# A two-layer encoder trunk: input, result and modulation weight with channels on partitions

## The chip, the cores and the metric

The kernel runs on one core of a Trainium2 chip, as one launch. The metric is the device time of that launch in microseconds (us). Six engine names occur: PE is TensorE's matrix multiply and PEld its loading of stationary operands, DVE is VectorE, ACT is ScalarE, POOL is GpSimd, SP is SyncE, which here only issues transfers (DMAs). A trailing q (SPq, ACTq) means the engine's instruction queue. On-chip memory has 128 partitions; a tile written 128x512 has 512 elements on each of them. PSUM is the memory that PE writes.

## The reference

```
c_act = silu(c)                                             # (1, 1024)
for l in range(2):
    mod = c_act @ w_ada[l] + b_ada[l]                       # (1, 6144)
    sh1, sc1, g1, sh2, sc2, g2 = split(mod, 6)
    h  = rms_norm(x, norm1_g[l]) * (1 + sc1) + sh1          # x: (1, 512, 1024)
    x  = x + g1 * mixer_sublayer(h, ...)                    # three token mixers, merged by gates
    h2 = rms_norm(x, norm2_g[l]) * (1 + sc2) + sh2
    gate, up = split(h2 @ w_ffn_in[l], 2)
    x  = x + g2 * ((silu(gate) * up) @ w_ffn_out[l])
return rms_norm(x, norm_f_g)
```

512 tokens, 1024 channels, everything in float32. `w_ada` is (2, 1024, 6144): 50 MB that are read once and used for a product with one vector, "the modulation". Its result is needed per channel. Most of the work is in the products with `w_in`, the three projections, `w_out` and the two FFN weights.

## The kernel before

**Layout of the body.** Inside the body the activations stand with channels on partitions: `k.xd` holds x as eight tiles of 128 channels by 512 tokens (`xt(kk)`). Every weight tile is split by `parts` into a high part (ACT, a cast) and a low part (DVE, a difference), and `three` multiplies with three matmuls, so one 128x128 block of a weight against 512 tokens is three matmuls of 512 columns. The matmuls of the whole kernel stand in PE's queue one behind the other; the body is a long stream of them, with the other engines preparing operands.

**The opening** (`first_products`, instructions of each engine in the order in which they are written, by `in_order`). The input arrives with tokens on partitions, as four tiles `xin` of 128x1024. ACT squares and sums each row (`sums`), DVE and POOL make the reciprocal root (`rstd`), DVE or ACT scale the rows (`scaled`), PE transposes them in 128x128 blocks (`turned`, L616) and they are copied to the channel layout `xr`. The modulation's first two groups (shift and scale of the first norm) are needed at once: for each channel tile kk a block of 1024x128 of `w_ada` is loaded twice (`fw`, once for each group, in pieces of 512 bytes); `columns` multiplies the one by `cact` on POOL and folds it to two 128x128 blocks (three POOL instructions, L624 and L626), and does the other with eight DVE instructions (L631, L633); `folded` adds over partitions with matmuls against a column of ones (L640). `tile` then makes shift and scale, applies them (L646, L648, L651), `split` makes the high and low part of h (L338, L339), and `products` runs the 18 matmuls of tile kk against the first three column blocks of `w_in` (banks `L0A0b`). From kk = 4 on `raw_x` puts transposes of the unscaled input between the matmuls (L656), so that `k.xd` has x in channel layout for the residual. The loads are issued by SP three tiles ahead; the buffer of a `w_in` block (`raw`, three of them) is reissued once the block has been split.

**The other ten groups of the modulation** (`mod_steps`) run in the background of the body, as 160 steps in the list `bg`. `weight`, which issues every weight load, also pops one or two steps (`k.rate`) while `k.ahead` allows it: two behind each weight load in the merge part of a layer, one in the FFN. A step loads 128 rows by 512 columns of `w_ada` (`wr`, 256 KB, two buffers, SP) and adds them, times `cact` for that partition, to `acc` on DVE (L208, L210). After eight steps, `fin` transposes `acc` with four PE transposes into PSUM (`mt`, L216), and DVE sums along rows (L218) and adds the bias (L220).

**Small vectors** (`arow`, `crow`, `prow`: biases, gains, bounds) are loaded as rows and turned by PE transposes.

**The seams.** Between sub-layers `boundary` runs the last two column blocks by halves of the tokens and the norm beside them: `squares` and `half_norm` (squares on ACT, sums over channels by matmuls with a column of ones, L423, the root on POOL, L352, then a diagonal matrix `dg`, L428, whose product with ones, L433, has 1/rms of each token on all partitions: `bc`). At the end, `last_norm` stops `half_norm` at the fifth of its seven steps, transposes x back to tokens on partitions (L1165), scales by 1/rms and by the gain `gf` (DVE, L1166, four 128x512 for each half) and writes 128 rows of the result with each of four DMAs (L1169).

**Buffers.** `duo` tiles (8 KB on each partition) come from a pool of 16; in the second part of each layer a further pool, `late`, has `LATE_DUOS` of the same size.

Outside `first_products` and the seam, the order of each engine is chosen when the program is built, by a scheduler that goes by program order as priority.

Of the kernel before, what the change touches and what calls it, by code (L numbers as in the profile page):

```python
# [11 lines left out]
F32 = mybir.dt.float32  # L12
# [3 lines left out]
ALU = mybir.AluOpType  # L16
# [22 lines left out]
R_N2, R_LB, R_NA, R_NB, R_NC, R_BA = 0, 16, 24, 32, 40, 48  # L39
R_END = 56  # L40

R_N1 = 96
R_EARLY = 112

# [5 lines left out]
LATE_DUOS = 4  # L50
# [66 lines left out]
def trunk_kernel(ctx: ExitStack, tc: tile.TileContext, a, out):  # L117
# [80 lines left out]
    def mod_steps(l, g):  # L198

        st = {}  # L200

        def row(hlf, kk):
            t = wp.tile([P, 512], F32, tag="ada", name=f"wr{l}_{g}_{hlf}_{kk}", bufs=2)
            c0 = g * DM + hlf * 512
            tc.keep_in_program_order(nc.sync.dma_start(t, a["w_ada"][l, kk * P:(kk + 1) * P, c0:c0 + 512]))
            if kk == 0:
                st["acc"] = wk.tile([P, 512], F32, tag="acc", name=f"acc{l}_{g}_{hlf}", bufs=1)
                nc.vector.tensor_scalar_mul(st["acc"], t, cact[:, 0:1])  # L208
            else:
                nc.vector.scalar_tensor_tensor(st["acc"], t, cact[:, kk:kk + 1], st["acc"],  # L210
                                               op0=ALU.mult, op1=ALU.add)

        def fin(hlf):
            ps = obank(f"mt{l}_{g}_{hlf}")
            for j in range(4):
                nc.tensor.transpose(ps[:, j], st["acc"][:, j * P:(j + 1) * P], ident)  # L216
            m = mod[l][:, g, hlf * 4:hlf * 4 + 4]
            nc.vector.tensor_reduce(m, ps, op=ALU.add, axis=AX.X)  # L218
            c0 = l * 48 + g * 8 + hlf * 4
            nc.vector.tensor_add(m, m, acol[:, c0:c0 + 4])  # L220
            if hlf:
                mod_finish(l, g)

        def step(hlf, kk):
            row(hlf, kk)
            if kk == KD - 1:
                fin(hlf)

        return [lambda hlf=hlf, kk=kk: step(hlf, kk) for hlf in range(2) for kk in range(KD)]
# [307 lines left out]
    def first_products():  # L537


        crow, arow = tmp("crow", (P, P)), tmp("arow", (P, P))  # L540
# [118 lines left out]
        for c in range(NCH):  # L659
            sums(c)  # L660
# [698 lines left out]
```

## Time and profile before

| | |
|---|---|
| median of three runs | 2006.54 us (2003.65 to 2008.01) |
| the profiled execution | 2004.59 us, its span 2002.8 us |
| PE busy | 1939.2 us, 97% |
| DVE / ACT / POOL busy | 1105.5 / 779.2 / 208.4 us |
| DMA | 231.95 MB, mean 116 GB/s |

"Busy" is the time in which an engine has an instruction in flight, "idle before" the time for which it stood still ahead of an instruction, with the event that ended it. The page cuts the span into 40 slices of 50 us. The opening is the first two of them, the merge parts of the layers lie at about 440 to 640 us and 1420 to 1610 us, the end is the last slice. A chain of waits, followed back from the last instruction, tells which work set the end.

### The profile page before, as it was taken

The page shows a single profiled execution, that of the slowest core. Times are in us where ns is not written, and L with a number is a line of the kernel's source. Part 1 is how long each engine was busy: PE and PEld are TensorE (multiplying, and loading weights), DVE is VectorE, ACT ScalarE, POOL GpSimd, SP SyncE. Part 2 cuts the span into 40 slices and gives each one's busy share as a digit, 9 for nine tenths or more (in the row PEclk, how much of TensorE's full clock was granted, in tenths as well). Part 3 has the DMA queues.
Part 4 walks back from the last instruction along what each step waited for, and adds up shares of the span by engine and source line. Part 5 has one row for each costly group of instructions (what it writes and reads, how often), then busy time and mean ns, then how long its engine had stood idle before and what let it go on. Part 6 is the DMA issues. An engine that isn't in the chain of part 4 may idle for free.

```text
span 2002.8 us, 32664 instructions
## 1 busy us (share of the span) xinstructions
PE 1939.2 (97%) x13507; PEld 1626.2 (81%) x13507; DVE 1105.5 (55%) x1797; ACT 779.2 (39%) x1298; POOL 208.4 (10%) x202
## 2 busy tenths in 40 slices
PE   5999999999999999999999999989999999999998
PEld 4898887777888888888889888777878888888887
DVE  7566576756635544453354756775764464434324
ACT  3543455633233433332244443654423353333222
POOL 6121011011110100000011201110111110000000
PEclk7999999999999999999999999999999999999999
DMA  8433212326633344443343322222564333333332
GB/s 248 144 100 92 77 57 85 107 97 190 187 95 118 103 129 155 139 145 116 116 125 89 105 76 67 75 93 78 178 195 122 95 122 126 111 99 101 101 95 79
DMA packets 208997, 231.95 MB, mean 116 GB/s; under 512 B 10720, under 2 KB 185104, under 8 KB 207824
## 3 DMA queue, kind: packets, MB, share of 16 engines
q1 hardware_dynamic: 207056, 224.80, 36.5%
q0 software_dynamic: 1504, 4.47, 0.8%
q8 instruction: 106, 1.74, 0.4%
q10 hardware_dynamic: 288, 0.58, 0.1%
q14 instruction: 43, 0.35, 0.1%
HBM read 221.43 MB, written 6.29 MB: 114 GB/s over the span
## 4 chain that ended last, share of the span: by engine, by line
PE 59%; issue 23%; DVE 7%; DMA 7%; ACT 1%; POOL 1%; SPq 0%; DVEq 0%; POOLq 0%; ACTq 0%
DMA wr<-w_ada 6%; DVE acc L210 1%; PE L0A0b L283 1%; PE L0A0b L284 1%; PE L0A0b L285 1%; DVE fw L633 1%; DMA fw<-w_ada 1%; PE L1fo2b L284 1%; PE L1fo1b L284 1%; PE L1fo0b L284 1%; PE L1fo1b L285 1%; PE L1fo0b L285 1%; PE L1fo2b L285 1%; PE L1fo2b L283 1%; PE L1fo1b L283 1%
## 5 line engine op out<-in xcount | busy, mean ns | idle before, releaser
L210 DVE SCALAR_TENSOR_TENSOR acc<-wr,cact,acc 128x512 f32<-128x512 f32 x140 | 106.1, 758 | 172.8 <-DMA wr<-w_ada 172.4
L352 POOL TENSOR_TENSOR L1h0r<-L1h0r,mhalf 128x2 f32<-128x2 f32 x1 | 1.1, 1079 | 348.4 <-DVE L1h0r L351 348.4
L352 POOL TENSOR_TENSOR fin0r<-fin0r,mhalf 128x2 f32<-128x2 f32 x1 | 0.7, 695 | 347.8 <-DVE fin0r L351 347.8
L338 ACT CAST L0hid<-L0fs 128x512 fp32r<-128x512 f32 x22 | 13.7, 622 | 31.9 <-DVE L0fs L1288 31.4
L633 DVE SCALAR_TENSOR_TENSOR fw<-fw,cact 128x128 f32<-128x128 f32 x48 | 23.2, 550 | 0.0
L218 DVE TENSOR_REDUCE mod<-mt 128x4 f32<-128x512 f32 x20 | 13.7, 686 | 15.0 <-PE mt L216 15.0
L640 PE MATMUL fm<-ones,fw 128*128 128x1 f32 x64 | 10.1, 278 | 11.9 <-DVE fw L633 9.1
L640 PEld LDWEIGHTS fm<-ones,fw 128*128 128x128 f32 x64 | 10.2, 237 | 13.9 <-DVE fw L633 10.1
L216 PE MATMUL mt<-ident,acc 128*128 128x128 f32 x80 | 13.3, 290 | 7.0 <-DVE acc L210 6.9
L1264 POOL TENSOR_TENSOR L1ma<-L1ma,L1sgb 128x512 f32<-128x512 f32 x6 | 10.1, 1704 | 92.9 <-DVE L1sgb L1263 92.9
L216 PEld LDWEIGHTS mt<-ident,acc 128*128 128x128 f32 x80 | 10.0, 148 | 11.4 <-issue 8.2
L651 ACT ACTIVATE xr<-xr,mod,gmul 128x512 f32<-128x512 f32 x8 | 6.5, 815 | 32.1 <-DVE gmul L648 32.1
L1264 POOL TENSOR_TENSOR L0ma<-L0ma,L0sgb 128x512 f32<-128x512 f32 x6 | 9.6, 1605 | 88.8 <-DVE L0sgb L1263 61.3
L624 POOL TENSOR_TENSOR fw<-fw,cact 128x1024 f32<-128x1024 f32 x8 | 17.0, 2120 | 11.9 <-DMA fw<-w_ada 11.9
L338 ACT CAST L1hid<-L1fs 128x512 fp32r<-128x512 f32 x22 | 13.7, 622 | 11.1 <-DVE L1fs L1288 10.0
L1264 POOL TENSOR_TENSOR L0ma<-L0ma,L0sgc 128x512 f32<-128x512 f32 x8 | 12.8, 1602 | 48.9 <-DVE L0sgc L1263 48.9
L1264 POOL TENSOR_TENSOR L1ma<-L1ma,L1sgc 128x512 f32<-128x512 f32 x8 | 12.4, 1559 | 47.1 <-DVE L1sgc L1263 47.1
L626 POOL TENSOR_TENSOR fw<-fw 128x512 f32<-128x512 f32 (+1 forms) x16 | 17.0, 1064 | 1.3
L339 DVE TENSOR_TENSOR L0hid<-L0fs,L0hid 128x512 fp32r<-128x512 f32 x22 | 15.1, 688 | 0.9
L339 DVE TENSOR_TENSOR L1hid<-L1fs,L1hid 128x512 fp32r<-128x512 f32 x22 | 15.2, 691 | 0.6
L767 DVE TENSOR_TENSOR L1AK<-L1AK,L1AG 128x1024 f32<-128x1024 f32 x12 | 14.6, 1216 | 0.7 <-POOL L1AG L759 0.7
L767 DVE TENSOR_TENSOR L0AK<-L0AK,L0AG 128x1024 f32<-128x1024 f32 x12 | 14.6, 1216 | 0.7 <-POOL L0AG L759 0.7
(5616 smaller groups left out, 6916.9 us busy)
## 6 DMA issues: line engine op xcount, KB each, us to landing
wr<-w_ada SPq DMA_DIRECT2D x160, 256.0 KB, 3.6
fw<-w_ada SPq DMA_DIRECT2D x16, 512.0 KB, 6.4
L0A0w<-w_in SPq DMA_DIRECT2D x8, 384.0 KB, 3.6
L0fo0w<-w_ffn_out SPq DMA_DIRECT2D x5, 512.0 KB, 4.0
L0fo1w<-w_ffn_out SPq DMA_DIRECT2D x5, 512.0 KB, 3.6
L0fo2w<-w_ffn_out SPq DMA_DIRECT2D x5, 512.0 KB, 3.5
L1hzw<-w_ffn_out SPq DMA_DIRECT2D x5, 512.0 KB, 3.5
L1fo0w<-w_ffn_out SPq DMA_DIRECT2D x5, 512.0 KB, 3.4
```

What stands on the lines that cost most here:

```text
L210: nc.vector.scalar_tensor_tensor(st["acc"], t, cact[:, kk:kk + 1], st["acc"], op0=ALU.mult, op1=ALU.add)
L216: nc.tensor.transpose(ps[:, j], st["acc"][:, j * P:(j + 1) * P], ident)
L283: nc.tensor.matmul(ps, ah, bh, start=first, stop=False, **kw)
L284: nc.tensor.matmul(ps, al, bh, start=False, stop=False, **kw)
L285: nc.tensor.matmul(ps, ah, bl, start=False, stop=last, **kw)
L338: nc.scalar.copy(h, src)
L339: return nc.vector.tensor_sub(dst[1][i // 2][:, i % 2], src, h.bitcast(F32))
L624: nc.gpsimd.tensor_mul(t, t, cact[:, :, None].to_broadcast([P, KD, P]))
L633: nc.vector.scalar_tensor_tensor(acc, t[:, j], cact[:, j:j + 1], acc, op0=ALU.mult, op1=ALU.add)
L640: nc.tensor.matmul(ps[:, g:g + 1], loads[kk][1 - g][:, j], ones[:, :1], start=j == 0, stop=j == 1)
L767: nc.vector.tensor_mul(kk, kk, crossed(t, s, d + 1, -d - 1, True))
L1264: nc.gpsimd.tensor_add(acc[i], acc[i], sg[i])
```

## The change

On the host, `x` and `w_ada` are transposed before the launch and the result behind it, and all small vectors are put side by side in one array `cols` of 128 x 176 in column form. In the kernel:

- x is loaded straight into `k.xd` (four DMAs of 512 KB). The transposes of `turned` and `raw_x`, and those of the small vectors, go.
- `cact` becomes 128x1024: c on all partitions. A piece of the modulation is then a dot product along rows: one DVE instruction over 128 channels by 512 inputs that also writes its row sum (`accum_out`). In `mod_steps` the steps stay 160, of the same 256 KB; `acc`, the transposes `mt` and the row reduction go. In the opening, each group's 128x1024 tile takes one DVE instruction with a sum (scale), or one POOL product and one ACT copy with a sum (shift).
- The first norm is done in channel layout: ACT squares, sums by matmuls with ones, POOL's root, the diagonal, `bc`; then for each tile one DVE instruction, one ACT instruction for the high part, one on DVE for the low part.
- The last norm runs `half_norm` to its end and multiplies in channel layout: eight DVE instructions of 128x256 for each half, and two DMAs of 512 KB.
- `LATE_DUOS` goes from 4 to 3; the pairs of `mg` and `hid` take one duo more each from the pool of 16, as does one tile of the seam between the layers.

```diff
-LATE_DUOS = 4
+LATE_DUOS = 3
...
+    cols = cst.tile([P, R_EARLY + R_END], F32, name="cols")
+    acol, pcol = cols[:, :R_EARLY], cols[:, R_EARLY:]
+    cact = cst.tile([P, DM], F32, name="cact")
...
     def mod_steps(l, g):
...
-        def fin(hlf):
-            ps = obank(f"mt{l}_{g}_{hlf}")
-            for j in range(4):
-                nc.tensor.transpose(ps[:, j], st["acc"][:, j * P:(j + 1) * P], ident)
...
+        def step(j, hlf):
...
+            t = wp.tile([P, 512], F32, tag="ada", name=f"wr{l}_{g}_{j}_{hlf}", bufs=2)
+            n0 = g * DM + j * P
+            tc.keep_in_program_order(nc.sync.dma_start(t, a["w_ada"][l, n0:n0 + P, hlf * 512:hlf * 512 + 512]))
+            nc.vector.scalar_tensor_tensor(t, t, 1.0, cact[:, hlf * 512:hlf * 512 + 512], op0=ALU.mult, op1=ALU.mult,
+                                           accum_out=st["sum"][:, hlf, j:j + 1])
...
     def first_products():
...
+        nc.scalar.dma_start(cact, a["c"].rearrange("o n -> (o n)").rearrange("(o n) -> o n", o=1).to_broadcast([P, DM]))
+        nc.scalar.dma_start(cols, a["cols"])
+        fresh_x("x")
+        for i in range(4):
+            nc.sync.dma_start(k.xd[i // 2][:, 2 * (i % 2):2 * (i % 2) + 2],
+                              a["x"][i * 2 * P:(i + 1) * 2 * P].rearrange("(j p) t -> p j t", p=P))
...
+            fd = duo(f"fw{kk}", shape=(P, 2, DM))
             for g in (1, 0):
...
+                nc.sync.dma_start(fd[:, g], a["w_ada"][0, g * DM + kk * P:g * DM + kk * P + P])
...
+        for i in range(2):
+            c, t = cact[:, i * 512:i * 512 + 512], tmp(f"cs{i}")
+            nc.scalar.activation(t, c, AF.Sigmoid)
+            nc.vector.tensor_mul(c, c, t)
+        def dots(kk):
+            fd = loads[kk][0]
+            nc.vector.scalar_tensor_tensor(fd[:, 1], fd[:, 1], 1.0, cact, op0=ALU.mult, op1=ALU.mult,
+                                           accum_out=mod[0][:, 1, kk:kk + 1])
+            nc.gpsimd.tensor_mul(fd[:, 0], fd[:, 0], cact)
+            nc.scalar.activation(fd[:, 0], fd[:, 0], AF.Copy, accum_out=mod[0][:, 0, kk:kk + 1])
+        def sums():
+            ps = obank("ssp", (P, 4))
+            for kk in range(KD):
+                sq = tmp(f"x0sq{kk}")
+                nc.scalar.activation(sq, xt(kk), AF.Square)
+                for c in range(NCH):
+                    nc.tensor.matmul(ps[:, c:c + 1], sq[:, c * P:(c + 1) * P], ones[:, :1], start=kk == 0 and c == 0,
+                                     stop=kk == KD - 1, skip_group_check=True)
+            r = rstd_of(ps, DM, "r0")
+            dg = tmp("x0dg", (P, 4, P))
+            nc.vector.tensor_tensor(dg, ident[:, None, :].to_broadcast([P, 4, P]),
+                                    r[:, :, None].to_broadcast([P, 4, P]), op=ALU.mult)
+            bc = obank("x0bc", (P, 4, P))
+            for c in range(NCH):
+                nc.tensor.matmul(bc[:, c], ones, dg[:, c], start=True, stop=True)
+            return bc.rearrange("p c t -> p (c t)")
+        bc = sums()
+        dots(0)
...
         def before(kk):
+            hl = [parts(loads[kk][1][:, :3, i * P:(i + 1) * P], f"L0A0w{kk}{i}") for i in range(2)]
             m = mod[0][:, 0:2, kk]
+            nc.vector.tensor_add(m, m, acol[:, 0:16].rearrange("p (g k) -> p g k", g=2)[:, :, kk])
             gm = gmul[0][:, 0, kk:kk + 1]
...
+            t, sh = tmp(f"x0t{kk}"), mod[0][:, 0, kk:kk + 1]
+            nc.vector.scalar_tensor_tensor(t, xt(kk), gm, bc, op0=ALU.mult, op1=ALU.mult)
+            hi, lo = h[0][kk // 2][:, kk % 2], h[1][kk // 2][:, kk % 2]
+            nc.scalar.activation(hi, t, AF.Identity, bias=sh)
+            nc.vector.scalar_tensor_tensor(lo, t, sh, hi.bitcast(F32), op0=ALU.add, op1=ALU.subtract)
+            if kk + 1 < KD:
+                dots(kk + 1)
             return hl
         def products(kk, i, hi, lo):
...
-            if kk >= NCH:
-                raw_x(kk - NCH, i)
...
     def last_norm(block, add):
...
+            for i in range(7):
+                bc = next(norm)
+            od = duo(f"out{hv}", shape=(P, KD, T // 2))
+            for kk in range(KD):
+                gf = pcol[:, R_NF + kk:R_NF + kk + 1]
+                nc.vector.scalar_tensor_tensor(od[:, kk], xt(kk)[:, half(hv)], gf, bc, op0=ALU.mult, op1=ALU.mult)
+                if kk % 4 == 3:
+                    dst = out[(kk - 3) * P:(kk + 1) * P, half(hv)].rearrange("(j p) t -> p j t", p=P)
+                    nc.sync.dma_start(dst, od[:, kk - 3:kk + 1])
```

More of the change, by code (lines that the diff above doesn't have):

```diff
@@ L200, in mod_steps @@
         st = {}
[L202 to L211, printed above, removed]
-        def fin(hlf):
-            ps = obank(f"mt{l}_{g}_{hlf}")
-            for j in range(4):
[L216 to L221, printed above, removed]
-                mod_finish(l, g)
[L224 to L229, printed above, removed]
+        def step(j, hlf):
+            if not st:
+                st["sum"] = sm.tile([P, 2, KD], F32, tag="msum", name=f"ms{l}_{g}")
+            t = wp.tile([P, 512], F32, tag="ada", name=f"wr{l}_{g}_{j}_{hlf}", bufs=2)
[3 more added lines that the diff above has]
+                                           accum_out=st["sum"][:, hlf, j:j + 1])
+            if j == KD - 1 and hlf:
+                m = mod[l][:, g]
+                nc.vector.tensor_add(m, st["sum"][:, 0], st["sum"][:, 1])
+                nc.vector.tensor_add(m, m, acol[:, l * 48 + g * 8:l * 48 + g * 8 + 8])
+                mod_finish(l, g)
+        return [lambda j=j, hlf=hlf: step(j, hlf) for j in range(KD) for hlf in range(2)]
     bg = []
@@ L591, in first_products @@
-        ss = sm.tile([P, 4], F32, tag="ss", name="ss0", bufs=3)
-        r = sm.tile([P, 4], F32, tag="rstd", name="r0", bufs=3)
-        xs = []
-        for c in range(0, NCH, 2):
-            d = duo(f"xs{c}", shape=(P, 2, DM))
-            xs += [d[:, 0], d[:, 1]]
-        def sums(c):
-            nc.scalar.activation(xs[c], xin[c], AF.Square, accum_out=ss[:, c:c + 1])
-        def rstd(c):
-            cc = slice(c, c + 1)
-            nc.vector.tensor_scalar(r[:, cc], ss[:, cc], 1.0 / DM, EPS, op0=ALU.mult, op1=ALU.add)
-            nc.gpsimd.tensor_tensor(r[:, cc], r[:, cc], mhalf[:, cc], op=ALU.pow)
@@ L635, in folded @@
-        def folded(kk):
-            ps = obank(f"fm{kk}", (P, 4))
-            for g in range(2):
-                for j in range(2):
-                    nc.tensor.matmul(ps[:, g:g + 1], loads[kk][1 - g][:, j], ones[:, :1], start=j == 0, stop=j == 1)
-            return ps
-        def tile(kk, ps):
+        for i in range(2):
[8 more added lines that the diff above has]
+            nc.scalar.activation(fd[:, 0], fd[:, 0], AF.Copy, accum_out=mod[0][:, 0, kk:kk + 1])
@@ L1340, in _arrays @@
     arrays.update(_constants())
+    t = lambda v: np.ascontiguousarray(np.asarray(v, dtype=np.float32).swapaxes(-1, -2))
+    arrays["x"], arrays["w_ada"] = t(inputs["x"][0]), t(inputs["w_ada"])
+    arrays["cols"] = t(np.concatenate([np.asarray(inputs[n], np.float32).reshape(-1, P) for n in _COLS]))
     wa = np.zeros((DEPTH, 2, 2, RANK, 2, 4 * C_DK), np.float32)
```

147 lines of the change are left out of this document (17 added, 130 removed).

## The prediction

> **What bounds the kernel now.** I read the page's slices first, then the stretches of the opening, then its timeline.
>
> ```profile
> span 2002.8 us, 32664 instructions
> PE   5999999999999999999999999989999999999998
> PEclk7999999999999999999999999999999999999999
> L210 DVE SCALAR_TENSOR_TENSOR acc<-wr,cact,acc 128x512 f32<-128x512 f32 x140 | 106.1, 758 | 172.8 <-DMA wr<-w_ada 172.4
> out<-out SPq DMA_DIRECT2D x4, 512.0 KB, 2.6
> ```
>
> PE has work in nearly every slice: the body is bound by the queue of matmuls, so what the change takes off PE is a gain at its full length, and what it adds to DVE costs nothing while DVE keeps ahead (for 172.4 us DVE only stood waiting for `wr`). The exceptions are the first slice and the end. The stretches of the opening:
>
> ```profile
> core 0: us, PE busy (x) PEld busy (x) DVE busy (x) ACT busy (x) POOL busy (x), PEclk, DMA share, GB/s
> 0.00:17.00 17.00, 6.94 (x34) 5.83 (x34) 8.23 (x22) 11.09 (x22) 9.06 (x15) 1.00 0.94 293
> 17.00:41.00 24.00, 12.01 (x34) 9.22 (x35) 21.31 (x32) 4.27 (x8) 16.30 (x13) 0.50 0.86 228
> 41.00:54.80 13.80, 11.02 (x57) 8.83 (x57) 12.85 (x25) 5.14 (x9) 8.61 (x7) 0.99 0.87 233
> 54.80:61.60 6.80, 6.80 (x20) 5.54 (x20) 6.76 (x14) 1.94 (x3) 5.19 (x4) 0.50 0.39 102
> 61.60:85.60 24.00, 24.00 (x136) 20.33 (x135) 11.90 (x35) 14.80 (x27) 0.00 (x0) 1.00 0.34 99
> ```
>
> From 17 to 61 us DVE is the full engine, together with POOL; only from 61.6 on does PE bind. The granted clock is half in two of these stretches. The timeline and the chain of waits give the prices:
>
> ```profile
> 5.84 0.19 ACT L599 ACTIVATION_READ_ACCUMULATOR xs<-xin 128x1 f32 x1
> 10.37 1.06 ACT L599 ACTIVATE xs<-xin 128x1024 f32<-128x1024 f32 x1 [0.26 <-DMA xin<-x]
> 12.96 1.90 POOL L624 TENSOR_TENSOR fw<-fw,cact 128x1024 f32<-128x1024 f32 x1
> 26.89 0.79 PE L283 MATMUL L0A0b<-h,L0A0w00h 128*128 128x512 f32 x1 [3.73 <-ACT h L338]
> 35.44 1.87 PE L640 MATMUL fm<-ones,fw 128*128 128x1 f32 x8 [3.14 <-DVE fw L633]
> 42.36 0.15 DVE L646 TENSOR_TENSOR mod<-fm,acol 128x2 f32<-128x2 f32 x1
> 42.55 1.67 DVE L648 SCALAR_TENSOR_TENSOR gmul<-mod,acol 128x1 f32<-128x1 f32 x1
> 44.25 0.81 ACT L651 ACTIVATE xr<-xr,mod,gmul 128x512 f32<-128x512 f32 x1 [2.40 <-DVE gmul L648]
> 47.55 1.04 PE L640 MATMUL fm<-ones,fw 128*128 128x1 f32 x8 [1.21 <-issue]
> 48.24 0.54 DVE L279 TENSOR_TENSOR L0A0w30l<-L0A0w,L0A0w30h 128x384 fp32r<-128x384 f32 x1
> 54.18 0.34 DVE L633 SCALAR_TENSOR_TENSOR fw<-fw,cact 128x128 f32<-128x128 f32 x1
> 54.36 1.50 PE L640 MATMUL fm<-ones,fw 128*128 128x1 f32 x8 [1.56 <-issue]
> 58.62 0.43 PE L0A0b L283
> 64.07 0.16 DVE L648 SCALAR_TENSOR_TENSOR gmul<-mod,acol 128x1 f32<-128x1 f32 x1
> 68.08 0.23 PE L0A0b L285
> 68.31 0.44 PE xtp L656 x4
> 68.75 0.79 PE fm L640 x8
> 85.60 0.12 PE L0Av0p L283
> ```
>
> The first product starts at 26.89 us, the next stage (`L0Av`) at 85.60. Of a tile's 18 products each takes 0.23 us at full clock and 0.43 at half: 4.2 or 7.7 us. DVE and POOL hinder each other: L648 takes 0.16 us alone, but 1.67 beside a POOL instruction, while L646, one of whose inputs is in PSUM, takes 0.15 then.
>
> **The opening after.** x comes in four DMAs as before (last quarter in ACT's hands at 10.4), with 0.5 MB of broadcast c beside it from ACT's queue; at 293 GB/s that adds 1.7 us, so x is complete at 12.1. ACT first needs c (two sigmoids), then eight squares of 128x512, some 0.63 each by L599 (1.06 for twice the size, part of it fixed), and is done by about 13.5. PE's sums are new: 8 matmul records for each tile, 0.79 to 1.87 us by clock, so 6 to 15 us in all from about 8 us on; I take 11, to 19. Root, diagonal and `bc` take some 2.7 us beyond that, but DVE is free after the diagonal, at about 20.7. Then, in DVE's order: the dot of tile 0 (128x1024: 0.34 us at 128 and 0.758 at 512 elements are 1.09 ns an element, so 1.3), two splits (1.1), bias and gain (0.3), the norm's product (0.75), ACT's high part (0.81): 25 us, and 1 for a collision with POOL. The first product starts at 26, hardly sooner (21 with sums of 6 us, 30 with 15).
>
> Then each tile costs DVE 2 x 0.54 (splits), 0.3 (bias, gain), 0.75, 0.75 (low part), 1.3 (next dot) = 4.2 us, and it stands 0.95 for ACT's high part, since the low part waits for it and the dot is queued behind: 5.1. ACT has two casts, the high part and a summing copy (1.06 + 0.19), 2.9; POOL one product of 1.90; DMA 2 x 512 + 384 KB, 4.8 us at 293 GB/s. So DVE still sets the pace. All its instructions but the norm's product read two SBUF tensors and stand aside for POOL like L648, so of POOL's 1.90 I charge half: 6.0 us for each tile (5.1 without collisions; 7.7 should PE stay at half clock). End: 26 + 7 x 6.0 + 0.7 + 4.2 = 72.9, against 85.6: a gain of 12.7, between 24 (21 + 35.7 + 4.9 = 61.6) and a loss of 3 (30 + 53.9 + 4.9 = 88.8). What goes from PE is 8 x 0.79 for `fm` and 8 x 0.44 for `xtp`, 9.8 us: that is why 61.6 to 85.6 shortens at all. The six loads of small rows leave SP; SP's other order stays, and `raw` is still what it waits for. `cols` and c stand in ACT's queue ahead of its first work, inside the 1.7.
>
> The Trainium skill (TensorE: Matmul & The Clock Gate, Part 1) says that the clock falls to half after an idle window of about 3.4 us. The rows differ: 1.21 us of idle at 46 us left it full, 1.56 us at 53 us was followed by half clock until 61.6. Per tile PE will idle about 1.8 us; by the page it stays at full clock and the last tile takes 4.2, by the rows it may take 7.7, 3.5 later.
>
> **The background steps.** Four transposes cost 0.44 us of the queue (`xtp`, same shape), 20 times: 8.8 us for certain. PE also waited for them:
>
> ```profile
> PE mt L216 <- DVE acc L210: 6.9, 5, 2.4
> 1495.63 1.09 PE L216 MATMUL mt<-ident,acc 128*128 128x128 f32 x4 [2.40 <-DVE acc L210]
> 1496.72 0.43 PE L1mgb2b L283
> 455.00:525.00 70.00, 66.91 (x301) 54.36 (x300) 49.71 (x76) 21.08 (x36) 9.20 (x6) 1.00 0.64 196
> 1440.00:1500.00 60.00, 55.40 (x245) 45.13 (x244) 38.63 (x62) 15.85 (x27) 6.26 (x4) 0.97 0.66 200
> ```
>
> PE's transposes stood behind the last step of a group, which stood behind a transfer; the one wait of 2.40 us also cost a spell of half clock (0.43 instead of 0.23), 1.7 us. Without `mt` nothing on PE waits for a step, except through DVE's splits that stand behind it. DVE is busy in 71% and 64% of these stretches and four split weights are in stock, so I take 14 of 8.8 + 6.9 + 1.7 = 17.4, with 8.8 as the other end. A step's DVE price with a row sum is not in the trace: bounds are 0.758 us (L210) and 0.758 + 0.19 (ACT's separate read of its sum); I take the lower, 0.2 more is covered by DVE's waits for `wr`. The 20 row reductions were off the path.
>
> **The end.** The last half's chain before:
>
> ```profile
> 1992.31 0.48 DVE L367 SCALAR_TENSOR_TENSOR L1x<-finzb,mod,L1x 128x256 f32<-128x256 f32 x1
> 1992.79 1.36 DVE out L1166 x2
> 1994.07 0.41 DVE L419 TENSOR_TENSOR finacc<-finacc,fin1sq 128x256 f32<-128x256 f32 x1
> 1994.63 0.58 PE L423 MATMUL fin1tp<-ones,finacc 128*128 128x1 f32 x4 [0.42 <-DVE finacc L419]
> 1995.55 0.70 POOL L352 TENSOR_TENSOR fin1r<-fin1r,mhalf 128x2 f32<-128x2 f32 x1 [4.36 <-DVE fin1r L351]
> 1996.28 2.91 DVE L1166 SCALAR_TENSOR_TENSOR out<-fo,fin1r,gf 128x512 f32<-128x512 f32 x4 [0.88 <-POOL fin1r L352]
> ```
>
> Added behind the root: diagonal (0.4, the size of L419), `bc` (0.5, as L423's four records), and eight instructions of 0.48 (L367's shape and inputs) for 2.91: 3.84. Together 1.8. The first half's outputs, which already held up the second half's sum (1992.79), become 3.84 us long: up to 2.4 more, or 1.4 less if they come earlier. Twelve transposes leave PE ahead of the last sum: 0.5 to 1.3. The last DMA stays 512 KB (2.6). I take +2 (-0.5 to +4).
>
> `LATE_DUOS`: at the seam between the layers x (2), `hid` (8), the held weights (2) and h (4) fill the 16 duos; the last tile comes when the first `hid` pairs have been multiplied, which PE does before the halves begin. That covers it; without the cover it is one stretch of half-width products, 48 x 0.12 = 6 us.
>
> **Sum.** 2004.59 - 12.7 - 14 + 2 = 1979.9, against the profiled execution, which stands 0.1% below the median 2006.54. I say 1980.
>
> **Rivals.** (1) Row sums at half rate. A doubled price per element adds 1.1 us to the opening's dot: 27 + 7 x 7.1 + 4.9 = 81.6, a gain of 4; in the steps the slack that held the 5.2 us of waits is used up, so 8.8 remain: 2004.6 - 4 - 8.8 + 2 = 1993.8. For it: no DVE row sum is in the trace. Against: L210 has two float32 inputs and runs at 1.09 ns an element. The Trainium skill (Vector Engine (DVE) Microarchitecture Reference, Points that are easy to get wrong) says it of this kind: "halves throughput — both read ports consumed, none for accumulator readback". Without a sum, L210 contradicts it; with one, no row can tell. Chance 0.11.
> (2) The opening gains nothing, because each tile takes 7.7 us (clock at half, or DVE behind POOL): 2004.6 - 0 - 14 + 2 = 1992.6. For it: 1.67 against 0.16 for L648. Against: POOL's instructions fall from three to one a tile. 0.10.
> (3) Slower: half-rate sums, and the chain of steps holds the splits. Place: the merge parts, 80 steps at two for each weight, where SP reissues a `wr` buffer only behind its DVE step. Price 0.56 us a step: 45, on top of (1): 2038.8. It decides against the change from 10.8/80 = 0.14 us a step on PE's path. Against: DVE is idle 30% there. 0.04.
> (4) No collisions and all waits gone: 2004.6 - 24 - 17.4 = 1963.2. 0.06.
>
> **How the numbers follow.** My forecast has 0.69: 1968 to 1991 by its own bounds. Range 1963 to 1995: it takes in (1), (2) and (4) and leaves out (3) and some mishaps. 0.2% (4 us) is what a measurement can tell: faster 0.93, same 0.03, slower 0.04.
>
> **What would show it.** `L0Av` starting at 66 to 80 us, DVE over 80% busy from 25 us on, steps of about 6 us; no `mt`, no PE idle behind background steps, body otherwise of equal length; 2 us more from the last product to the end. Wrong it is made by a DVE row sum well over 0.95 us at 128x512, by PE sums lasting past 25 us, or by new waits for a duo.

## The result, and the profile after

The changed kernel takes 2036.58 us (median of 4 runs, 2034.12 to 2039.13), the kernel before beside it 2005.1: a ratio of 1.0158 [1.0133, 1.0183]. It is 1.6% slower, where 1980 us had been forecast. Its profiled execution has these lines on its page:

```profile
span 2037.3 us, 32251 instructions
PE 1941.5 (95%) x13344; PEld 1618.6 (79%) x13344; DVE 1076.7 (53%) x1894; ACT 771.1 (38%) x1289; POOL 193.8 (10%) x183
L207 DVE SCALAR_TENSOR_TENSOR wr<-wr,cact 128x512 f32<-128x512 f32 x160 | 111.9, 705 | 294.8 <-DMA wr<-w_ada 294.6
wr<-w_ada SPq DMA_DIRECT2D x160, 256.0 KB, 4.1
```

The third line is the one to compare with L210 of before. The step's instruction got no dearer (705 ns where L210 had 758), but VectorE's idle time ahead of it went from 172.4 to 294.6 us. The chain of waits shows who stood behind VectorE. PE now waits for low parts of weights (L265, `...l`), 17 times, 19.7 us in all; the longest three are

```profile
PE L1mga2b L270 <- DVE L1mga2w41l L265: 3.3, 1, 3.3
PE L0fo0b L270 <- DVE L0fo0w201l L265: 2.5, 1, 2.5
PE L0mgc1b L270 <- DVE L0mgc1w41l L265: 2.5, 1, 2.5
```

Before, there were two such waits, of 1.1 us together. Where the time went, by the first product of each stage in the timelines (us from the start; three further kernels are described below):

| stage that begins | before | changed | `new_steps` | `late_dots` | `all_three` |
|---|---|---|---|---|---|
| opening (`L0A0b`) | 26.9 | 36.6 | 27.4 | 36.4 | 24.7 |
| attention of layer 0 (`L0Av0p`) | 85.4 | 82.7 | 84.5 | 78.9 | 65.1 |
| output projection of layer 0 (`L0wo0b`) | 605.2 | 611.8 | 611.8 | 589.4 | 570.1 |
| layer 1 (`L1hzb`) | 1008.3 | 1028.0 | 1020.1 | 988.9 | 969.6 |
| output projection of layer 1 (`L1wo0b`) | 1578.6 | 1610.4 | 1601.4 | 1545.9 | 1527.8 |
| last norm (`fin0tp`) | 1989.7 | 2019.8 | 2010.8 | 1955.4 | 1937.2 |
| end of the span | 2002.8 | 2037.3 | 2024.3 | 1973.2 | 1952.0 |

Between the rows of the changed kernel and before: the opening is 2.7 us shorter (12.7 had been forecast), attention and merge of layer 0 are 9.3 longer, its feed-forward part 13.1, attention and merge of layer 1 12.1, its feed-forward part 1.7 shorter, the end 4.4 longer. The sum is the 34.5 us between the two spans. The stretches that became longer by 9 us or more are those in which background steps run. The start of A's V moves between executions even where the opening is the same: it lies between 78.9 us (`late_dots`) and 82.7 us (the changed kernel), while the first product stands at 36.3 to 36.6 us in all of them.

One such wait in the timeline of the changed kernel, with the load queue, VectorE and PE (start, duration, what was done; in brackets the idle time ahead of it and who ended it):

```profile
937.29 0.69 DVE L207 SCALAR_TENSOR_TENSOR wr<-wr,cact 128x512 f32<-128x512 f32 x1 [3.71 <-DMA wr<-w_ada]
937.91 0.69 DVE L265 TENSOR_TENSOR L0fo0w161l<-L0fo0w,L0fo0w161h 128x512 fp32r<-128x512 f32 x1
938.62 0.37 SPq L252 DMA_DIRECT2D L0fo1w<-w_ffn_out  x1
939.04 0.50 SPq L206 DMA_DIRECT2D wr<-w_ada  x1
944.42 0.69 DVE L207 SCALAR_TENSOR_TENSOR wr<-wr,cact 128x512 f32<-128x512 f32 x1 [5.49 <-DMA wr<-w_ada]
945.24 0.42 DVE L265 TENSOR_TENSOR L0fo0w201l<-L0fo0w,L0fo0w201h 128x256 fp32r<-128x256 f32 x1
945.71 0.66 PE L270 MATMUL L0fo0b<-L0hid,L0fo0w201l 128*128 128x512 f32 x1 [2.52 <-DVE L0fo0w201l L265]
946.17 0.63 PE L271 MATMUL L0fo0b<-L0hid,L0fo0w201h 128*128 128x512 f32 x1
949.16 0.47 PE L269 MATMUL L0fo1b<-L0hid,L0fo1w00h 128*128 128x512 f32 x1
949.70 0.39 PE L271 MATMUL L0fo1b<-L0hid,L0fo1w00h 128*128 128x512 f32 x1
```

Read it as a loop. The split at 937.91 ends at 938.60 and with that frees a `raw` buffer; at 938.62 SP can issue the next weight, and behind it the next step's half row, at 939.04. The step that needs this half row is next in VectorE's queue, so VectorE stands for 5.49 us. The split `L0fo0w201l` could have run meanwhile: ACT had finished the high part of the same weight at 936.61. It stands behind the step and starts only at 945.24. PE has no low part to multiply and waits 2.52 us. Then it runs at half pace until 949.2 (products 0.43 us apart, 0.23 after; the granted clock of this stretch is 0.53). A weight of four row blocks and 256 columns gives PE 24 products of 0.23 us, 5.5 us; the loop of split, issue, landing, step and split takes as long or longer, and VectorE cannot get ahead.

Before, the same loop had a brake that helped. There is one accumulator, which the next half group may write only after PE's four transposes have read it:

```profile
837.08 0.50 SPq L205 DMA_DIRECT2D wr<-w_ada  x1
839.06 0.50 SPq L205 DMA_DIRECT2D wr<-w_ada  x1
849.00 0.48 DVE L208 TENSOR_SCALAR acc<-wr,cact 128x512 f32<-128x512 f32 x1
850.06 0.75 DVE L210 SCALAR_TENSOR_TENSOR acc<-wr,cact,acc 128x512 f32<-128x512 f32 x1
```

These half rows were issued at 837.08 and 839.06 and used at 849.00 and 850.06, 11 to 12 us later, with no idle time ahead of them. The steps were held, VectorE did splits meanwhile, and the data lay there when the steps came.

The opening after:

```profile
8.06 13.81 PE L567 MATMUL ssp<-ones,x0sq 128*128 128x1 f32 x64 [8.06 <-ACT x0sq L565]
23.18 11.00 POOL L557 TENSOR_TENSOR fw<-fw,cact 128x1024 f32<-128x1024 f32 x4
23.22 2.83 DVE L571 TENSOR_TENSOR x0dg<-ident,r 128x512 f32<-128x512 f32 x1 [1.16 <-POOL r L338]
25.98 3.39 DVE L555 SCALAR_TENSOR_TENSOR fw<-fw,cact 128x1024 f32<-128x1024 f32 x1
29.30 2.68 DVE L265 TENSOR_TENSOR L0A0w00l<-L0A0w,L0A0w00h 128x384 fp32r<-128x384 f32 x1
31.90 2.69 DVE L265 TENSOR_TENSOR L0A0w01l<-L0A0w,L0A0w01h 128x384 fp32r<-128x384 f32 x1
36.58 0.79 PE L269 MATMUL L0A0b<-h,L0A0w00h 128*128 128x512 f32 x1 [8.39 <-ACT h L594]
82.69 0.28 PE L269 MATMUL L0Av0p<-L0Av0w00h,h 128*128 128x256 f32 x1
```

The sums by PE last to 21.9. The root is POOL's and stands ahead of POOL's products in its order; when it is done, four products that had been waiting run back to back, and VectorE's four instructions of that time take 11.6 us. Later in the same stage the dot takes 1.22 and a split 0.55, and the diagonal takes 0.69 in a kernel below, so the four would need 3.0. And the end:

```profile
2022.02 0.48 DVE L353 SCALAR_TENSOR_TENSOR L1x<-finzb,mod,L1x 128x256 f32<-128x256 f32 x1
2022.56 3.22 DVE L1062 SCALAR_TENSOR_TENSOR out<-L1x,cols,fin0bc 128x256 f32<-128x256 f32 x8
2025.70 0.41 DVE L405 TENSOR_TENSOR finacc<-finacc,fin1sq 128x256 f32<-128x256 f32 x1
2030.12 3.22 DVE L1062 SCALAR_TENSOR_TENSOR out<-L1x,cols,fin1bc 128x256 f32<-128x256 f32 x8 [1.38 <-PE fin1bc L419]
```

The eight output products of the first half stand ahead of the second half's sum (L405), which PE waits for, in all 3.7 us.

### The profile page after: what moved, and what is told of

Read it like the earlier page. It is cut to its first block, busy times and chain, and to the rows that moved or that the text cites. A ratio compares the mean times of both kernels' runs of the same rounds, so it can differ in the third digit from the quotient of the medians.

```text
span 2037.3 us, 32251 instructions
## 1 busy us (share of the span) xinstructions
PE 1941.5 (95%) x13344; PEld 1618.6 (79%) x13344; DVE 1076.7 (53%) x1894; ACT 771.1 (38%) x1289; POOL 193.8 (10%) x183
## 5 line engine op out<-in xcount | busy, mean ns | idle before, releaser
L207 DVE SCALAR_TENSOR_TENSOR wr<-wr,cact 128x512 f32<-128x512 f32 x160 | 111.9, 705 | 294.8 <-DMA wr<-w_ada 294.6
L324 ACT CAST L0hid<-L0fs 128x512 fp32r<-128x512 f32 x22 | 13.7, 621 | 86.1 <-DVE L0fs L1184 86.0
L557 POOL TENSOR_TENSOR fw<-fw,cact 128x1024 f32<-128x1024 f32 x8 | 21.2, 2659 | 19.8 <-DMA fw<-w_ada 19.8
L567 PE MATMUL ssp<-ones,x0sq 128*128 128x1 f32 x64 | 13.8, 352 | 8.1 <-ACT x0sq L565 8.1
L567 PEld LDWEIGHTS ssp<-ones,x0sq 128*128 128x128 f32 x64 | 13.7, 332 | 8.1 <-ACT x0sq L565 8.1
L324 ACT CAST L1hid<-L1fs 128x512 fp32r<-128x512 f32 x22 | 13.7, 623 | 16.0 <-DVE L1fs L1184 15.1
L1160 POOL TENSOR_TENSOR L1ma<-L1ma,L1sgc 128x512 f32<-128x512 f32 x8 | 12.7, 1598 | 55.7 <-DVE L1sgc L1159 55.7
L594 ACT ACTIVATE h<-x0t,mod 128x512 fp32r<-128x512 f32 x8 | 5.8, 722 | 29.0 <-DVE x0t L592 29.0
L674 DVE TENSOR_TENSOR L1AQ<-L1AQ,L1AG 128x1024 f32<-128x1024 f32 x12 | 14.6, 1214 | 0.0
L674 DVE TENSOR_TENSOR L0AQ<-L0AQ,L0AG 128x1024 f32<-128x1024 f32 x12 | 14.6, 1213 | 0.0
L555 DVE SCALAR_TENSOR_TENSOR fw<-fw,cact 128x1024 f32<-128x1024 f32 x8 | 14.1, 1763 | 0.0
L595 DVE SCALAR_TENSOR_TENSOR h<-x0t,mod,h 128x512 fp32r<-128x512 f32 x8 | 10.1, 1258 | 6.2 <-ACT h L594 6.2
L668 POOL TENSOR_TENSOR L0AqT<-L0AG 128x1024 f32<-128x1024 f32 x2 | 8.0, 4016 | 54.6 <-DVE L0AG L858 54.6
```

What stands on the lines that cost most here:

```text
L207: nc.vector.scalar_tensor_tensor(t, t, 1.0, cact[:, hlf * 512:hlf * 512 + 512], op0=ALU.mult, op1=ALU.mult, accum_out=st["sum"][:, hlf, j: ...
L324: nc.scalar.copy(h, src)
L555: nc.vector.scalar_tensor_tensor(fd[:, 1], fd[:, 1], 1.0, cact, op0=ALU.mult, op1=ALU.mult, accum_out=mod[0][:, 1, kk:kk + 1])
L557: nc.gpsimd.tensor_mul(fd[:, 0], fd[:, 0], cact)
L567: nc.tensor.matmul(ps[:, c:c + 1], sq[:, c * P:(c + 1) * P], ones[:, :1], start=kk == 0 and c == 0, stop=kk == KD - 1, skip_group_check=True)
L594: nc.scalar.activation(hi, t, AF.Identity, bias=sh)
```

## The experiments

Each expectation says what its theories are; A is the loop above, VectorE standing at the head of its queue for a transfer. Ratios are against runs of the kernel before in the same comparison. The medians of these runs lie between 2000.8 and 2005.1 us, so times from two comparisons can differ by 4 us for that alone; a difference between them is best taken from the ratios.

**Which part costs.** `new_steps` is the kernel before with the change's background steps alone (weights turned, c along the free dimension, three late duos):

```diff
-                nc.vector.scalar_tensor_tensor(st["acc"], t, cact[:, kk:kk + 1], st["acc"],
-                                               op0=ALU.mult, op1=ALU.add)
...
+            nc.vector.scalar_tensor_tensor(t, t, 1.0, crep[:, hlf * 512:hlf * 512 + 512], op0=ALU.mult, op1=ALU.mult,
+                                           accum_out=st["sum"][:, hlf, j:j + 1])
```

> The kernel before, with only the background steps of the change (row sums against c on all partitions, no acc, no mt; the weight's transpose as a further input; LATE_DUOS 3); opening and end stay as before. Theory A (the steps: VectorE now stands before each of 160 steps for its transfer, while the old steps, kept back by the single acc buffer, came in bunches whose data had landed): about 2005 + 28 = 2033 us, VectorE's wait for wr near 295 us instead of 172. Theory B (the opening or the end, or the smaller late pool in it, costs the time): within 6 us of 2005, since the opening is the old one; if the pool alone, 2030 with a wr wait near 172.

Measured: 2027.65 us against 2000.79, ratio 1.0137 [1.012, 1.0155].

```profile
DVE wr L210 <- DMA wr<-w_turn: 284.8, 106, 5.0
```

The steps alone cost 27 us, with nearly the waits of the whole change.

`old_steps` is the reverse: the changed kernel with the steps of before (accumulator, transposes, weights as they were).

```diff
-            t = wp.tile([P, 512], F32, tag="ada", name=f"wr{l}_{g}_{j}_{hlf}", bufs=2)
+            t = wp.tile([P, 512], F32, tag="ada", name=f"wr{l}_{g}_{hlf}_{kk}", bufs=2)
...
+                nc.vector.scalar_tensor_tensor(st["acc"], t, ccol[:, kk:kk + 1], st["acc"],
+                                               op0=ALU.mult, op1=ALU.add)
```

> The changed kernel, with the background steps of before (acc, four transposes mt for each half group, the untransposed weight as a further input); opening, end and LATE_DUOS 3 stay changed. Theory A: 2037 - 28 = about 2008, wr wait near 172 us. Theory C (the duo that moved from the late pool makes new waits): stays above 2025. If the opening and end are worth what their landmarks in the trace say (-2.7 and +1.5 to +4.4 us), 2004 to 2010.

Measured: 1999.52, ratio 0.9996 [0.9982, 1.0009]; VectorE's waits for `wr` are back at 157.9 us. All else in the change (layouts, opening, end, one late duo less) comes out at nothing in sum. In times of the first comparison the ratio means 2004 us, the low end of what was expected.

**Is it the landing?** In `contig` each step's half rows lie as one block of 256 KB in HBM instead of 128 rows of 2 KB at a pitch of 4 KB:

```diff
-            tc.keep_in_program_order(nc.sync.dma_start(t, a["w_ada"][l, n0:n0 + P, hlf * 512:hlf * 512 + 512]))
+            tc.keep_in_program_order(nc.sync.dma_start(t, a["w_steps"][l, g * 8 + j, hlf]))
```

> The changed kernel, but each step's 128x512 block of the weight lies in one piece of 256 KB in memory, where it was half rows of 2 KB at a pitch of 4 KB. Theory D (the transposed layout lands later: median 4.1 us against 3.6 before, and that is the loss): landing back at 3.6 us and some 28 us faster, about 2009. Theory A: the landing may move, but VectorE still stands for each step; within 6 us of 2037.

Measured: 2024.31, ratio 1.0108 [1.0091, 1.0125]: by the ratios some 10 us less than the changed kernel, not 28, but also more than the 6 us that theory A allowed. The median landing went from 4.1 to 3.9 us, the waits to 279.9. A shorter landing helps a little as long as VectorE stands for it; it isn't the cause.

**Take the instruction from the head of the queue.** In `late_dots` the transfers keep their places in the load queue, but the step's VectorE instruction is queued behind the split of the weight that was loaded with it:

```diff
+            def dot():
+                nc.vector.scalar_tensor_tensor(t, t, 1.0, cact[:, hlf * 512:hlf * 512 + 512], op0=ALU.mult,
+                                               op1=ALU.mult, accum_out=st["sum"][:, hlf, j:j + 1])
...
+            k.dots.append(dot)
...
-            nc.vector.tensor_sub(lo, raw, hi.bitcast(F32))
+            low = nc.vector.tensor_sub(lo, raw, hi.bitcast(F32))
+        if k.dots:
+            with tc.issue_after(low.ins):
+                k.dots.pop(0)()
```

> The changed kernel; each step's VectorE instruction is queued behind the split of the weight with which it was loaded, instead of where the scheduler put it, two weights earlier. Nothing else changes, the buffers stay two. Theory A: VectorE's wait for wr falls from 295 us to under 80, the waits of TensorE for low parts in the merge and FFN parts go, and the removed transposes show at last: 1990 to 2005. If the loss lies elsewhere: 2030 or more.

Measured: 1977.59, ratio 0.9882 [0.9866, 0.9898]: by the ratios 55 us below the changed kernel, 1.2% faster than before, and 12 us better than the best that was expected. From its page and its waits:

```profile
span 1973.2 us, 32404 instructions
PE 1915.6 (97%) x13344; PEld 1610.9 (82%) x13344; DVE 1086.2 (55%) x1894; ACT 775.1 (39%) x1289; POOL 192.5 (10%) x183
DVE wr L209 <- DMA wr<-w_ada: 14.8, 14, 1.8
wr<-w_ada SPq DMA_DIRECT2D x160, 256.0 KB, 2.9
```

VectorE executes the same work and 294.6 us of waits become 14.8; PE has no wait for a split left. Of the 64.1 us between the spans 25.9 are in PE's busy time, for the same 13344 instructions: PE lost time not only by standing but by half pace afterwards (mean granted clock 0.985 in the changed kernel, 0.994 here).

The cross-check is `no_wait`: transfers stay, and the VectorE instruction reads c and a column of ones instead of the landed rows, so the modulation's values are left out.

```diff
-            nc.vector.scalar_tensor_tensor(t, t, 1.0, cact[:, hlf * 512:hlf * 512 + 512], op0=ALU.mult, op1=ALU.mult,
+            c = cact[:, hlf * 512:hlf * 512 + 512]
+            nc.vector.scalar_tensor_tensor(c, c, 1.0, ones[:, :1].to_broadcast([P, 512]), op0=ALU.mult, op1=ALU.mult,
                                            accum_out=st["sum"][:, hlf, j:j + 1])
```

> The changed kernel, with each background step's transfer kept at its place and its VectorE instruction kept at its place in VectorE's order, but reading the condition vector and a column of ones instead of the landed half rows (the modulation's values are left out). Theory A (the 28 to 35 us are PE's time behind VectorE standing for a transfer at the head of its in-order queue): the wait is gone, so as with the delayed instructions, 1974 to 1985. Theory B (the steps cost by what VectorE executes, 0.69 us + 0.08 us a step, or by the transfers beside the weights on the load queue): nothing of that is changed, 2025 to 2037.

Measured: 1973.76, ratio 0.9851 [0.9835, 0.9868]. One reservation: with nothing to wait for, these instructions also moved forward in VectorE's order and run in bunches (the first starts at 73.3 us, not after 320), and a transfer's buffer is no longer held until VectorE has read it. But all 160 of them are executed and all the transfers are made, with the median landing of the changed kernel, 4.1 us, and nothing is lost. In `late_dots` the same instructions run among the splits and nothing is lost either. Theory B, the price of the steps and transfers themselves, falls by the two together.

**Was before's brake a help?** `acc2` is the kernel before with a second accumulator; the room for it comes from `LATE_DUOS` 3, as in the changed kernel:

```diff
-                st["acc"] = wk.tile([P, 512], F32, tag="acc", name=f"acc{l}_{g}_{hlf}", bufs=1)
+                st["acc"] = wk.tile([P, 512], F32, tag="acc", name=f"acc{l}_{g}_{hlf}", bufs=2)
```

> The kernel before with its own steps and two accumulators instead of one (room for it from LATE_DUOS 3, which moved nothing in the earlier comparison of new and old steps). Theory A as it now stands (in before the one accumulator, freed only by PE's four transposes, held the first steps of each half group for 11 to 12 us, so that the next ones found their rows landed and VectorE caught up): without the hold more steps stand for their transfer, waits on wr above 220 us instead of 172.4, and the time goes to 2008 to 2025. Rival: the hold was itself a cost, and the steps gain or nothing moves: 1992 to 2006, waits no higher than 180 us.

Measured: 2041.46, ratio 1.0196 [1.0173, 1.0219].

```profile
DVE acc L210 <- DMA wr<-w_ada: 231.1, 96, 5.4
DVE acc L208 <- DMA wr<-w_ada: 28.1, 13, 5.1
```

One buffer more, which takes away a wait, costs 38 us. PE waits 20.0 us for splits, as in the changed kernel, and is busy 15.4 us longer than before with the same 13507 instructions. This reproduces the loss with none of the change's instructions. The expectation's sign was right and its size too small by 16 us or more. `acc2_late` queues its accumulations behind the splits, as `late_dots` does; `late_before` does it to the kernel before with one accumulator:

```diff
+            def add():
...
+                    nc.vector.scalar_tensor_tensor(st["acc"], t, cact[:, kk:kk + 1], st["acc"],
+                                                   op0=ALU.mult, op1=ALU.add)
...
+            k.dots.append(add)
```

> The kernel before with two accumulators (2041.5 as it was) and each accumulation queued behind the split of the weight loaded with it, as in the changed kernel with delayed steps. Theory A (the second accumulator costs only by taking away what held the steps back, and VectorE then stands for the transfers): the whole loss goes, 1988 to 1999, like the delayed steps with one accumulator (1996.4). Rival (the second accumulator's loss lies in the transposes' new places or in the smaller late pool): 2015 to 2041.

> The kernel before with its own steps, each accumulation queued behind the split of the weight that is loaded with it. Theory A with before's waits harmless (the single accumulator, free only after the transposes, already held half of the steps back, and PE stood for the splits in few places): 1995 to 2003, no change to be told. Rival: before loses by the same wait, in part: its 172.4 us of waits against the changed kernel's 294.6 us, which cost some 28 us, would be worth up to 16 us: 1985 to 1990, and then part of what the delayed steps gain is not the change's own.

Measured: `acc2_late` 1992.06, ratio 0.9943 [0.9926, 0.9959], with 33.1 us of waits: the whole loss of the second accumulator goes, and a little more. `late_before` 1996.4, ratio 0.9968 [0.9957, 0.9979], with 57.9 us of waits: inside the first expectation's range, but with an interval that excludes no change. So delaying the steps is worth some 6 us in the kernel before, too. By which path is not shown: VectorE's waits for `wr` fall from 172.4 us, but PE's waits for splits only from 1.1 to 0.4 us and those for the transposes from 6.9 to 6.2. Of `late_dots`' 23 us, about 6 are therefore to be had without the change; against `late_before` the change with delayed steps is worth 17 us by the ratios, 21.4 between the two profiled spans (1973.2 against 1994.6).

**Is any landing effect left?** `late_contig` is `late_dots` with the blocks of `contig`.

```diff
+            tc.keep_in_program_order(nc.sync.dma_start(t, a["w_steps"][l, g * 8 + j, hlf]))
...
+            k.dots.append(dot)
```

> The changed kernel with delayed steps (1977.6) and each step's half rows laid out as one block of 256 KB (which alone gave the changed kernel back about 10 us). Theory A (an earlier landing helps only while VectorE stands for it): no wait is left that it could shorten, 1974 to 1980. Rival D (the rows' layout slows the weights' own transfers on the same engines): the same 8 to 12 us come back again, 1965 to 1970.

Measured: 1975.45, ratio 0.986 [0.9835, 0.9885], against 0.9882 [0.9866, 0.9898] for `late_dots`: no difference to be told. The layout costs only while VectorE stands for it.

**The opening.** All three kernels stand on `late_dots`. `open_dve` computes both dot products on VectorE, none on POOL, tile 0's ahead of the sums; the low part of each tile's h is queued behind the next tile's dots:

```diff
-            nc.gpsimd.tensor_mul(fd[:, 0], fd[:, 0], cact)
-            nc.scalar.activation(fd[:, 0], fd[:, 0], AF.Copy, accum_out=mod[0][:, 0, kk:kk + 1])
+            nc.vector.scalar_tensor_tensor(fd[:, 0], fd[:, 0], 1.0, cact, op0=ALU.mult, op1=ALU.mult,
+                                           accum_out=mod[0][:, 0, kk:kk + 1])
...
-        bc = sums()
         dots(0)
+        bc = sums()
```

> The changed kernel with delayed steps (1977.6 in the last comparison), and in the opening both dot products on VectorE (2 x 1.30 us a tile), none on POOL, tile 0's ahead of the squares' sums. Theory P (the first product came at 36.4 us and not at 26 because POOL's four waiting products ran back to back and slowed VectorE's next four instructions 2 to 5 times): first product at 27 to 29, pace 5.6 to 5.8 us a tile by VectorE, the products of A's V at 72 to 75 where they were at 78.9, 1971 to 1974. Rival L (the arrival of the tiles, 1.4 MB each, sets the pace of the opening): the first product is earlier, but A's V starts at 77 to 80 all the same, 1975 to 1979.

Measured: 1962.25, ratio 0.9794 [0.9779, 0.9808], 15 us less than `late_dots` (18 by the ratios), more than any theory had.

```profile
23.20 0.69 DVE L580 TENSOR_TENSOR x0dg<-ident,r 128x512 f32<-128x512 f32 x1 [1.16 <-POOL r L347]
26.72 1.22 DVE L564 SCALAR_TENSOR_TENSOR fw<-fw,cact 128x1024 f32<-128x1024 f32 x1
27.61 0.80 PE L278 MATMUL L0A0b<-h,L0A0w00h 128*128 128x512 f32 x1 [1.60 <-ACT h L603]
68.89 0.28 PE L278 MATMUL L0Av0p<-L0Av0w00h,h 128*128 128x256 f32 x1
```

The root comes at the same time (23.20 against 23.22), and without POOL's four products the diagonal takes 0.69 us instead of 2.83 and the first product starts 9 us earlier. Theory P holds for most of it: the diagonal and the two splits together are 6.4 us shorter; the rest comes from tile 0's dot, which took 3.4 us there, 1.2 of them its own length, and now runs ahead of the sums. 10 of the 13.7 us between the two spans are there by the start of A's V; the rest come later, and no run isolates them.

`open_both` also adds the squares on VectorE, but behind tile 0's dots:

```diff
-                for c in range(NCH):
-                    nc.tensor.matmul(ps[:, c:c + 1], sq[:, c * P:(c + 1) * P], ones[:, :1], start=kk == 0 and c == 0,
-                                     stop=kk == KD - 1, skip_group_check=True)
+                if kk == 0:
+                    acc = sq
+                else:
+                    nc.vector.tensor_add(acc, acc, sq)
```

> As the one before, and the squares added on VectorE as they come, with 4 products by ones behind them instead of 32 (13.81 us of PE at half clock in the opening). Theory S (those products held the sums by 5 us): the root at about 18 us, first product at 22 to 24, the products of A's V at 67 to 70, 1966 to 1970. Rival L (arrival): first product no earlier than 27 or A's V at 73 to 80, 1971 to 1979.

Measured: 1960.82, ratio 0.9792 [0.9776, 0.9809], no gain over `open_dve`. It did not test its theory: VectorE did the seven additions in one block from 16.46 to 21.8 us, behind the dots, so the sums came as late as with 32 products. `open_sums` has the additions ahead of the dots:

```diff
-        dots(0)
         bc = sums()
...
+            dots(0)
             r = rstd_of(ps, DM, "r0")
```

> The opening with both dot products on VectorE (1962.3) and the squares added on VectorE ahead of tile 0's dot products, where the last comparison had them behind these (its sums came at 23.7 us, no earlier than with 32 products). Theory S (the sums hold the first product): root at 18 to 19 us, first product at 22 to 24, and A's V at 64 to 67 where it was at 68.9, 1957 to 1960. Rival L (the DMA engines, 93 to 97% busy to 40 us, set when the tiles are there): the first product is earlier, A's V stays at 68 to 71, 1961 to 1964.

Measured: 1956.62, ratio 0.977 [0.9746, 0.9793].

```profile
20.12 0.69 DVE L584 TENSOR_TENSOR x0dg<-ident,r 128x512 f32<-128x512 f32 x1 [1.16 <-POOL r L347]
24.53 0.79 PE L278 MATMUL L0A0b<-h,L0A0w00h 128*128 128x512 f32 x1 [1.59 <-ACT h L606]
65.47 0.28 PE L278 MATMUL L0Av0p<-L0Av0w00h,h 128*128 128x256 f32 x1
```

Three us earlier at the first product, and still 3.4 at A's V: these three us were held by the sums, not by the arrival of the tiles.

**The end.** `end_order` (on `late_dots`) queues the first half's eight output products behind the second half's sum, in the gaps of its chain:

```diff
+        with tc.issue_after(k.sum.ins):
+            outs(0, bc0, (0, 1, 2))
+        next(norm)
+        next(norm)
+        with tc.issue_after(k.rs.ins):
+            outs(0, bc0, (3, 4))
+        next(norm)
+        with tc.issue_after(k.dg.ins):
+            outs(0, bc0, (5, 6, 7))
```

> The changed kernel with delayed steps, and the eight output products of the first half queued on VectorE behind the second half's sum, three, two and three of them in the gaps of its chain. Theory E (the end's loss is that the second half's sum stands behind the first half's eight outputs): the end, from the second half's last product to the last store, is 2.5 to 3 us shorter, 1974 to 1976. Rival: the chain through PE, POOL and the stores sets it whatever the order: within 0.5 us of 1977.6 in the trace's end.

Measured: 1974.97, ratio 0.9859 [0.9836, 0.9882]. By time alone that is no difference from `late_dots`; its execution also had a slower opening (82.5 us to A's V against 78.9). The end itself, in the timeline:

```profile
1963.66 0.48 DVE L362 SCALAR_TENSOR_TENSOR L1x<-finzb,mod,L1x 128x256 f32<-128x256 f32 x1
1964.63 0.42 DVE L414 TENSOR_TENSOR finacc<-finacc,fin1sq 128x256 f32<-128x256 f32 x1 [0.48 <-ACT fin1sq L411]
1968.98 3.22 DVE L1070 SCALAR_TENSOR_TENSOR out<-L1x,cols,fin1bc 128x256 f32<-128x256 f32 x8 [0.20 <-PE fin1bc L428]
```

From the last update of x to the last outputs it takes 5.32 us; in the changed kernel it took 8.10 (2022.02 to 2030.12), so 2.8 us come back, as theory E had it.

**All three together.** `all_three` has the orders of `late_dots`, `open_sums` and `end_order`.

> The changed kernel with all three orders mended: the steps' instructions delayed behind a split, the opening's dot products on VectorE behind the added squares, the second half's sum ahead of the first half's outputs. The parts have no stage in common: 1956.6 by the last comparison less 2.8 us of the end (as the end's trace showed), 1951 to 1956. Rival: what the opening gains is given back later, or the end's 2.8 us only move to the stores: 1956 to 1962.

Measured: 1953.68, ratio 0.9747 [0.9732, 0.9761]: 2.5% faster than before, 4.1% below the changed kernel, within the expected 1951 to 1956. The parts add up.

```profile
span 1952.0 us, 32288 instructions
DVE wr L209 <- DMA wr<-w_ada: 17.9, 16, 2.5
```

## Why the prediction was wrong, step by step

**The background steps: the failing step.** Forecast: a gain of 14. Measured by the profiles from A's V to the last norm: a loss of 32.8 (1937.1 us against 1904.4). The step that failed is the sentence that 0.2 us more a step "is covered by DVE's waits for `wr`", with "for 172.4 us DVE only stood waiting" read as slack. A wait at the head of an in-order queue is no cover for what is queued behind it; it is a delay of it. What lay behind were the splits, which the prediction named ("except through DVE's splits that stand behind it") and then dropped, arguing from VectorE's busy share of 64 and 71%. It also counted the removed transposes as pure gain. They held the accumulator, and so the steps, until their data had landed; `acc2` shows that taking this hold away costs 38 us by itself. The gains were real: with the steps delayed in both kernels, the new ones are 20.3 us better in the same stretch (1876.5 us in `late_dots`, 1896.8 in `late_before`), near the listed 17.4.

**The step's price** was right: 0.70 us and 0.08 for the read of the sum, within 0.758 to 0.95. Rival (1), half rate, is refuted. For a VectorE operation of this kind with two SBUF inputs that are not bf16, the Trainium skill (Vector Engine (DVE) Microarchitecture Reference, Points that are easy to get wrong) has halved throughput; the trace shows nothing of it (with a row sum 705 ns at 128x512 and 1.22 us at 128x1024, without one 758 ns at 128x512).

**Rival (3)**, slower, had the right place and nearly the measured time, 2038.8, at a chance of 0.04. Its price was wrong in kind: 0.56 us a step from half-rate sums, which do not exist, and on the merge parts alone. What bound was the landing within the loop, in the feed-forward part of layer 0 as well. Its threshold (0.14 us a step on PE's path) asked the right question; the argument against it, "DVE is idle 30% there", was the same mistake.

**The opening.** Forecast 72.9 to A's V, a gain of 12.7 from 85.6 (before, the first product of A's V is at 85.4); measured 82.7, a gain of 2.7. That is inside the bounds of the opening, a gain of 24 and a loss of 3, and the same opening gave 78.9 us in `late_dots`. The pace was right (5.8 us a tile against 6.0: 82.69 - 36.58 = 46.1 over 8). The start was mis-sized: 36.6 instead of 26, beyond its bound of 30. PE's sums took 13.8 us instead of 11, and "1 for a collision with POOL" was 8.6: four products had piled up behind the root. `open_sums` shows the first and `open_dve` most of the second.

**The end.** Forecast +2 (-0.5 to +4); measured +4.4 from `fin0tp` to the end (17.5 against 13.1 us). The mechanism, first outputs holding up the second half's sum, was named, and its price was mis-sized: all eight came first, 3.2 us. `end_order` returns 2.8.

**`LATE_DUOS`**: nothing, as forecast (`old_steps` has three late duos and loses nothing).

**The clock.** The prediction weighed rows of 1.21 us of idle (clock stayed full) and 1.56 us (half) against the idle window of about 3.4 us (Trainium skill, TensorE: Matmul & The Clock Gate, Part 1). The changed kernel sides with the rows: after the 2.52 us of idle shown above came 3.5 us at half pace, so that window is too long here, and 1.35 us left full pace:

```profile
916.26 0.50 PE L270 MATMUL L0fo0b<-L0hid,L0fo0w01l 128*128 128x512 f32 x1 [1.35 <-DVE L0fo0w01l L265]
916.60 0.39 PE L271 MATMUL L0fo0b<-L0hid,L0fo0w01h 128*128 128x512 f32 x1
916.84 0.40 PE L269 MATMUL L0fo0b<-L0hid,L0fo0w01h 128*128 128x512 f32 x1
```

**Sum.** Against the forecast the profiled execution (2039.1) is 59 us worse: opening 10.0, steps 46.8, end 2.4. In these executions 11 us of the steps' part stay without a settled cause: from A's V to the last norm `new_steps` loses 21.9 us where the changed kernel loses 32.8, with the same layout of the half rows, and `contig` loses 23.6. The half rows' layout can be part of it, and so can the order in which steps and splits fall within the loop; `late_contig` shows only that nothing of it is left once VectorE no longer stands. By their ratios (1.0158 and 1.0137) the changed kernel and `new_steps` are only 4 us apart, and the intervals overlap, so a part of the 11 us can belong to the two executions.

## What to carry to other kernels

An engine's idle time in front of a transfer is slack only for what is ahead of it in its queue; before counting on it, name the instruction queued behind the waiting one and who waits for that. Put background work that waits for its own load behind the urgent work of the same round, not ahead of it. Before removing a buffer or a dependency that holds work back, ask whether that hold is what lets the data arrive in time.

## What was not expected of the hardware

In `late_dots` the steps' transfers also landed sooner, at a median of 2.9 us instead of 4.1, without any change to their layout. The end of VectorE's waits alone does not explain it: in `no_wait`, where it does not wait for them either, the median stays 4.1. No run isolates the reason. A POOL product of 128x1024 beside VectorE stretched VectorE's instructions with two SBUF inputs to between 2.8 and 4.9 times their length (1.22 to 3.39, 0.55 to 2.68), and took 2.75 us itself where 1.90 had been read before. Four POOL products at 1.90 and VectorE's four instructions at their 3.0 us are 10.6 us together, near the 11.0 and 11.6 us that the two engines took: an estimate from these rows, by which they took turns. And the first products of the opening ran 0.43 us apart, from 36.58 to 41.0 us in the changed kernel, while the granted clock (1.00 in this stretch, ahead of the DMA share) is given as full:

```profile
36.00:41.00 5.00, 4.42 (x10) 3.38 (x11) 3.81 (x8) 2.85 (x6) 0.00 (x0) 1.00 0.85 294
37.17 0.63 PE L270 MATMUL L0A0b<-h,L0A0w00l 128*128 128x512 f32 x1
37.59 0.63 PE L271 MATMUL L0A0b<-h,L0A0w00h 128*128 128x512 f32 x1
```

PE's sums ahead of them took 13.8 us for 64 records, 1.73 us for eight, nearer to the 1.87 us that eight such records had taken at half clock than to the 0.79 at full, and the column gives 1.00 there as well. So the clock column alone does not show every spell at half pace.
